# A gMLP output projection computed for two token blocks at a time with Strassen's seven products, in a one-core decoder trunk of split fp32 matmuls

## The chip, the core and the metric

The kernel runs on one core of a Trainium2 chip. The metric is the device time of one execution in microseconds. Three runs of the kernel before took 2581.13, 2582.24 and 2583.32 us; the median is 2582.24 us. All times below are of the kernel before.

## What is computed

A two-layer trunk for 2048 prompt tokens and 32 sample tokens with shared weights, model width 1024. Layer A (the one that changes) is a gated MLP over chunks of 128 positions:

```python
def chunk_gmlp(h, w_in, ln_g, ln_b, w_s, b_s, w_out):
    u, v, z = jnp.split(h @ w_in, 3, axis=-1)          # 3 x 2048 columns
    v = layernorm(v, ln_g, ln_b)
    ...
    s = jnp.einsum('hts,bnshd->bnthd', ws, vc) + bias  # mixes 128 positions, 8 heads
    gated = u * s.reshape(bn, seq_len, EXP_A) * jax.nn.silu(z)
    return gated @ w_out, v                            # (tokens, 2048) @ (2048, 1024)
...
x = x + rmsnorm(out, norm_post[i])
```

Layer B is an S5 state-space mixer and a GLU; the change leaves it as it is.

## The kernel before, in words

**Arithmetic.** Each fp32 product is made of three matmuls: an operand is split into a high part (ScalarE cast, L69) and a low part (VectorE subtraction, L70), and `mm3` (L62) accumulates hi·hi, hi·lo and lo·hi in a PSUM bank. The profile calls the weights' parts `whi` and `wlo`, those of the gate output `gs`, those of the normed input `hn`. `weight` (L72) loads 512 KB from DRAM into `wst` (2 buffers, SyncE's queue, L82) and splits it. PSUM has 6 banks `mm` for products and 2 `aux` for transposes.

**Order of layer A.** The prompt is four blocks `b` of 512 tokens; block 3 carries the 32 sample tokens too. For each block:
- `v_phase` (L250): v = hn·wv in four column groups n of 512, each group into four banks, copied by ScalarE into one `vq` tile of the pool `vg` (L274), with statistics by VectorE (L275).
- `uz_phase` (L329): 16 steps `db` of 128 features: u and z (112 matmuls with the spatial product, 12.0 us), then a = silu(z)·u (L344, L345), the spatial product `wsp`·`vq`, and gate output `gq` = spatial·a (L358, L365). `gq` is four tiles of `vg` (feature-major, 4 x 512 tokens each). In blocks 0 and 1 each step also makes tables for layer B (`cpow`, L681): GpSimd products, two small matmuls `aux<-oh,bsh`, a copy to `vt`, and for every second one eight DMAs `td<-vt` on SyncE's queue (L732).
- `out_phase` (L417): out = gated·w_out for the block through `tmajor` (L382): for each half h of the 1024 columns, 16 k of 128 features, four row tiles i, three matmuls of 128x512: 384 a block, in four banks. The four banks of a half are copied to `oq` by ScalarE and get their statistics by VectorE (`evac`, L154). Each operand tile `gs` is split just ahead of its use; the pool `gs` has two buffers.

The norm and transpose of the next block's input (`prep`, L126) run inside `out_phase` through a hook; the residual step of a block (`post`, L159: `xr` loaded, GpSimd or VectorE addition, store to x1d) runs in the next `v_phase`.

A scheduler in the framework sets the order on each engine; `later` and `behind` (L90 to L97) tie a load to an earlier weight load or split. Each queue is worked in order: what waits on SyncE's queue holds up every load behind it.

## Time and profile before

| | us |
|---|---|
| median of the runs | 2582.24 (2581.13 to 2583.32) |
| profiled execution | 2583.09 |
| its span | 2581.3 |
| TensorE (PE) busy | 2554.0, 99% |
| PE weight loads (PEld), beside PE | 2183.2, 85% |
| VectorE (DVE) busy | 1501.7, 58% |
| ScalarE (ACT) busy | 926.2, 36% |
| GpSimd (POOL) busy | 429.5, 17% |
| mean granted TensorE clock | 0.995 |

How to read it: the profile is of one execution, the span is what its trace covers, and the sum of the prediction is made against that execution's 2583.09 us. The matmuls are pipelined, so a duration of 0.39 us is that of one, and they start 0.227 us apart.

### The profile page before, as it was taken

The page shows a single profiled execution, that of the slowest core. Times are in us where ns is not written, and L with a number is a line of the kernel's source. Part 1 is how long each engine was busy: PE and PEld are TensorE (multiplying, and loading weights), DVE is VectorE, ACT ScalarE, POOL GpSimd, SP SyncE. Part 2 cuts the span into 40 slices and gives each one's busy share as a digit, 9 for nine tenths or more (in the row PEclk, how much of TensorE's full clock was granted, in tenths as well). Part 3 has the DMA queues.
Part 4 walks back from the last instruction along what each step waited for, and adds up shares of the span by engine and source line. Part 5 has one row for each costly group of instructions (what it writes and reads, how often), then busy time and mean ns, then how long its engine had stood idle before and what let it go on. Part 6 is the DMA issues. An engine that isn't in the chain of part 4 may idle for free.

```text
span 2581.3 us, 34682 instructions
## 1 busy us (share of the span) xinstructions
PE 2554.0 (99%) x13163; PEld 2183.2 (85%) x13163; DVE 1501.7 (58%) x2809; ACT 926.2 (36%) x1520; POOL 429.5 (17%) x624
## 2 busy tenths in 40 slices
PE   9999999999999999999999999999999999999998
PEld 8888888788888888887999877889888888888896
DVE  5955657745655755744633547417897346464645
ACT  3322443323443222532222344325556433434331
POOL 0345100455100000000100120000023212121220
PEclk9999999999999999999999999999999999999999
DMA  5333424343534454343322346537699545454533
GB/s 168 100 127 112 135 95 151 116 122 115 153 116 130 163 162 155 109 138 93 105 78 82 107 128 191 145 110 212 215 321 303 186 132 183 138 183 144 163 123 102
DMA packets 220631, 375.04 MB, mean 145 GB/s; under 512 B 59520, under 2 KB 135808, under 8 KB 220464
## 3 DMA queue, kind: packets, MB, share of 16 engines
q1 hardware_dynamic: 165728, 308.09, 37.6%
q0 software_dynamic: 13600, 39.90, 4.9%
q10 hardware_dynamic: 41136, 24.84, 3.4%
q8 instruction: 103, 1.69, 0.3%
q14 instruction: 64, 0.52, 0.1%
HBM read 311.64 MB, written 61.11 MB: 144 GB/s over the span
## 4 chain that ended last, share of the span: by engine, by line
PE 89%; DVE 5%; DMA 3%; issue 1%; ACT 1%; SPq 0%; POOL 0%; DVEq 0%; ACTq 0%; POOLq 0%
PE mm L60 85%; PE aux L60 3%; DMA x<-in_xp_dram 1%; DVE wlo L70 1%; PE aux L146 1%; DMA x<-x1d 1%; ACT junk L135 0%; DMA T<-td 0%; DMA Xo<-xd 0%; DVE nt L107 0%; DMA wst<-in_wib_dram 0%; ACT whi L69 0%; DVE o L175 0%; DVE nt L108 0%; DMA Xi<-xd 0%
## 5 line engine op out<-in xcount | busy, mean ns | idle before, releaser
L60 PE MATMUL mm<-hn,whi 128*128 128x512 f32 (+2 forms) x3840 | 1011.1, 351 | 0.0
L70 DVE TENSOR_TENSOR wlo<-wst,whi 128x1024 fp32r<-128x1024 f32 x400 | 516.3, 1292 | 536.0 <-ACT whi L69 520.6
L60 PEld LDWEIGHTS mm<-hn,whi 128*128 128x128 f32 x3840 | 671.6, 189 | 88.0 <-DVE a L345 0.2
L69 ACT CAST whi<-wst 128x1024 fp32r<-128x1024 f32 x400 | 419.7, 1050 | 860.4 <-PE mm L60 758.6
L60 PE MATMUL mm<-hn,wlo 128*128 128x512 f32 (+2 forms) x1920 | 673.2, 351 | 2.9 <-DVE wlo L70 2.9
L60 PEld LDWEIGHTS mm<-hn,wlo 128*128 128x128 f32 x1920 | 361.7, 188 | 48.4 <-DVE wlo L70 3.3
L60 PE MATMUL mm<-y,whi 128*128 128x512 f32 (+2 forms) x1280 | 333.8, 350 | 3.1 <-ACT y L69 2.9
L60 PE MATMUL mm<-whi,gs 128*128 128x512 f32 x1024 | 328.4, 393 | 2.2 <-ACT a L344 1.4
L60 PE MATMUL mm<-whi,hn 128*128 128x512 f32 x1024 | 324.4, 392 | 0.6 <-ACT hn L69 0.6
L60 PEld LDWEIGHTS mm<-y,whi 128*128 128x128 f32 x1280 | 224.7, 188 | 34.8 <-ACT y L69 3.6
L60 PEld LDWEIGHTS mm<-whi,gs 128*128 128x128 f32 x1024 | 191.6, 188 | 44.9 <-ACT a L344 1.7
L60 PEld LDWEIGHTS mm<-whi,hn 128*128 128x128 f32 x1024 | 192.6, 189 | 43.5 <-ACT hn L69 0.9
L60 PE MATMUL mm<-y,wlo 128*128 128x512 f32 (+2 forms) x640 | 223.1, 349 | 0.0
L60 PE MATMUL mm<-wlo,hn 128*128 128x512 f32 x512 | 200.2, 391 | 0.1
L60 PE MATMUL mm<-wlo,gs 128*128 128x512 f32 x512 | 199.8, 390 | 0.0
L70 DVE TENSOR_TENSOR gs<-gq,gs 128x512 fp32r<-128x512 f32 (+1 forms) x128 | 91.1, 714 | 133.7 <-ACT gs L69 133.4
L60 PE MATMUL mm<-whi,m 128*128 128x512 f32 x512 | 159.8, 389 | 0.0
L69 ACT CAST gs<-gq 128x512 fp32r<-128x512 f32 (+1 forms) x128 | 80.5, 629 | 190.3 <-PE mm L60 175.4
L60 PEld LDWEIGHTS mm<-y,wlo 128*128 128x128 f32 x640 | 120.8, 189 | 15.1
L60 PEld LDWEIGHTS mm<-wlo,hn 128*128 128x128 f32 x512 | 96.4, 188 | 21.5 <-DVE wlo L70 0.5
L358 DVE SCALAR_TENSOR_TENSOR gq<-mm,lng,Rp 128x512 f32<-128x512 f32 x64 | 47.9, 748 | 114.5 <-PE mm L60 114.5
L60 PEld LDWEIGHTS mm<-whi,m 128*128 128x128 f32 x512 | 96.1, 188 | 20.7
(287 smaller groups left out, 2624.0 us busy)
## 6 DMA issues: line engine op xcount, KB each, us to landing
wst<-in_wuz_dram SPq DMA_DIRECT2D x128, 512.0 KB
wst<-in_wv_dram SPq DMA_DIRECT2D x64, 512.0 KB
wst<-in_woa_dram SPq DMA_DIRECT2D x64, 512.0 KB
wst<-in_wg_dram SPq DMA_DIRECT2D x64, 512.0 KB
wst<-in_wib_dram SPq DMA_DIRECT2D x48, 512.0 KB
wst<-in_wob_dram SPq DMA_DIRECT2D x32, 512.0 KB
Xi<-xd SPq DMA_DIRECT2D x32, 272.0 KB
Xo<-xd SPq DMA_DIRECT2D x32, 272.0 KB
```

Of the source, the lines that this page charges most:

```text
L60: self.nc.tensor.matmul(out, lhsT, rhs, start=start, stop=stop)
L69: self.nc.scalar.copy(hi, src)
L70: return (e or self.nc.vector).tensor_tensor(lo, src, hi.bitcast(F32), SUB)
L146: nc.tensor.transpose(b[:, k * 128:k * 128 + P], x[:, o:o + 128], self.ident[:P, :P])
L358: nc.vector.scalar_tensor_tensor(g3, s3, self.lng[:, db:db + 1], R, MUL, ADD)
```

## The change

For the blocks (0,1) and (2,3), `out_pair` (new) replaces `out_phase`. The gate outputs of the two blocks are the upper and lower half of a 2x2 matrix of blocks (rows: even and odd block; columns: features k = 0..7 and 8..15), w_out a second one (features by column half). Strassen's scheme makes the four results from seven products instead of eight, each 8 k x 4 row tiles x 3 matmuls. In the order of the program, with the operand on the left:

| product | left operand | by | right operand |
|---|---|---|---|
| p1 | even(k) | loaded | w_out block |
| p6 | s2 = odd(k) - even(k) + odd(k+8) | GpSimd, then VectorE | `wtd` 2 |
| p2 | even(k+8) | loaded | w_out block |
| p7 | s3 = even(k) - odd(k) | GpSimd | `wtd` 1 |
| p5 | s1 = odd(k) + odd(k+8) | GpSimd, in place | `wtd` 0 |
| p3 | s4 = even(k) + even(k+8) - s1(k) | GpSimd, then VectorE | w_out block |
| p4 | odd(k+8) | in SBUF | `wtd` 3 |

- The even block's `gq` tiles go to DRAM (`gat`, `spill`, four writes of 1 MB a pair) and come back as tiles `ge` of 256 KB, 48 loads a pair, on SyncE's queue, in a ring of four. The sums are formed in the `ge` tiles.
- `combine_w` (new, in block 1, before its v_phase) makes the four sums of weights once on GpSimd: 32 loads of 256 KB, 32 additions of 128x512, 8 writes of 1 MB to `wtd`, all on GpSimd's queue, through tiles `tw` of the pool `vg`.
- A bank is no longer only copied: it is added by VectorE to the results it belongs to (p5 to two), and the statistics are then read from SBUF.
- `gs` has three buffers; `ge`, `gs` and the odd block's results are in a new pool `oc`, opened when the pair begins.
- The prep of blocks 1 and 3 moves into the `uz_phase` of blocks 0 and 2 (`prep_held`): ScalarE copies the transposes back to `x`, and `unhold` splits them into `hn` at the start of the odd block's `v_phase`. The residual steps of both blocks of a pair run after the pair: eight in block 2's `v_phase` (3, 3, 2), eight at the end of layer A.

In all 192 of the 1536 matmuls of 128x512 go, and 8 of the 64 weight loads of the four output projections.

```diff
+    def combine_w(self):
+        e, w = self.nc.gpsimd, self.I["woa"]
+        for kp in range(4):
+            for kk in range(2):
...
+                t = self.vg.tile([128, 4, 512], F32, tag="vg", name="tw", align_bytes=AL)
+                for i, (h, k) in enumerate(((0, kp), (1, kp), (1, kp + 4), (0, kp + 4))):
+                    e.dma_start(t[:, i], w[h, k][:, c])
+                b11, b12, b22, b21 = (t[:, i] for i in range(4))
+                e.tensor_tensor(b11, b12, b11, SUB)
+                e.tensor_tensor(b12, b22, b12, SUB)
+                e.tensor_tensor(b22, b22, b11, SUB)
+                e.tensor_tensor(b21, b22, b21, SUB)
+                e.dma_start(self.wtd[:, kp].rearrange("i p x -> p i x")[:, :, c], t)
+
+    def out_pair(self, s, hook):
...
+        oc = self.oc = self.tc.tile_pool(name="oc", bufs=2, reuse_waits="tile")
...
+        def even(k):
+            t = p.tile([128, 512], F32, tag="ge", name="ge", bufs=4)
+            self.later(t, self.gat[s][k])
+            return t
+        def s2(k):
+            t = even(k)
+            e.tensor_tensor(t, g(k), t, SUB)
+            v.tensor_tensor(t, t, g(k + 8), ADD)
+            return t
+        def s3(k):
+            t = even(k)
+            e.tensor_tensor(t, t, g(k), SUB)
+            return t
+        def s1(k):
+            e.tensor_tensor(g(k), g(k), g(k + 8), ADD)
+            return g(k)
+        def s4(k):
+            t, u = even(k), even(k + 8)
+            e.tensor_tensor(t, t, u, ADD)
+            v.tensor_tensor(t, t, g(k), SUB)
+            return t
...
+        for n, (pr, a, wsrc, asmp) in enumerate(plan):
+            bk = [self.bank() for _ in range(4)]
...
+            for kp in range(4):
+                hook(n * 4 + kp)
+                w = self.weight(wsrc(kp), (2, 512))
...
+                for k in ks:
+                    x = a(k)
+                    t = p.tile([128, 2, TB], F32R, tag="gs", name="gs", bufs=3, align_bytes=AL)
+                    self.split(t[:, 0], t[:, 1], x)
...
+                if kp < 3:
+                    for k in ks:
+                        for i in range(4):
+                            mm(i, k)
+                else:
+                    for i in range(4):
+                        for k in ks:
+                            mm(i, k)
+                        out(i, pr, bk[i])
...
             for b in range(NB):
+                if b % 2:
+                    self.unhold(hn, held)
+                    if b == 1:
+                        self.combine_w()
...
                 self.v_phase(b, hn, vhook)
```

The order on three queues, where the prediction speaks of it. First SyncE's queue at the end of block 1's `uz_phase`, where block 1's output projection (before) or the first pair (now) begins. `td<-vt` are the writes of the last tables, `wst` the weights, `x` the next block's input, `ge` the even block's gate output. Before:

```order
L97 DMA x<-in_xp_dram 128x1024 x2
L732 DMA td_92<-vt 16x4x128 x8
L82 DMA wst<-in_woa_dram 128x1024 x2
L732 DMA td_92<-vt 16x4x128 x8
L82 DMA wst<-in_woa_dram 128x1024 x11
```

And now:

```order
L97 DMA x<-in_xp_dram 128x1024 x2
L82 DMA wst<-in_woa_dram 128x1024
L912 DMA td_95<-vt 16x4x128 x8
L82 DMA wst<-in_woa_dram 128x1024
L82 DMA wst<-wtd 128x1024
L912 DMA td_95<-vt 16x4x128 x8
L97 DMA ge<-gat_74 128x512 x9
L82 DMA wst<-wtd 128x1024
```

The writes of the last tables stood behind the block's first four weight loads and nothing of its first products waited for them; now the first operand of the pair, `ge`, stands behind them, and it waits for all eight of SyncE's DMA counters as well, because `oc` takes over the memory of the tables' pool.

Second, VectorE in the first pair, from the end of p1 into p6 (`ge_5494` to `ge_5589` are p6's k = 0, 1, 2, ...; L478 is the VectorE part of s2, `gs<-ge` the low part of an operand):

```order
L478 TENSOR_TENSOR ge_5501<-ge_5501,gq_4460 128x512
L70 TENSOR_TENSOR gs_5453<-ge_5451,gs_5453 128x512
L478 TENSOR_TENSOR ge_5538<-ge_5538,gq_4460 128x512
L70 TENSOR_TENSOR gs_5498<-ge_5494,gs_5498 128x512
L70 TENSOR_TENSOR wlo_5535<-wst_5532,whi_5534 128x1024
L478 TENSOR_TENSOR ge_5545<-ge_5545,gq_4460 128x512
L478 TENSOR_TENSOR ge_5582<-ge_5582,gq_4880 128x512
L70 TENSOR_TENSOR gs_5505<-ge_5501,gs_5505 128x512
```

Before, VectorE had there one `wlo` and two `gs` for each pair of k and nothing else; now a sum stands between them for each k, and the sums of k = 3 and k = 4 (`ge_5545`, `ge_5582`) stand ahead of the low part of k = 1 (`gs_5505`).

Third, GpSimd's queue in the last step of block 0's `uz_phase` and the start of block 1's `v_phase`, where before it had only a `MEMSET vt` and one load (`oh` and `vt` belong to the tables, `tw` and `wtd` to `combine_w`; a tile's four additions are L441 to L444):

```order
L892 MEMSET vt_2722 16x4x112
L442 TENSOR_TENSOR tw_2870<-tw_2870 128x512
L442 TENSOR_TENSOR tw_2880<-tw_2880 128x512
L443 TENSOR_TENSOR tw_2850<-tw_2850 128x512
L443 TENSOR_TENSOR tw_2860<-tw_2860 128x512
L443 TENSOR_TENSOR tw_2870<-tw_2870 128x512
L443 TENSOR_TENSOR tw_2880<-tw_2880 128x512
```

```order
L444 TENSOR_TENSOR tw_2880<-tw_2880 128x512
L439 DMA tw_2890<-in_woa_dram 128x512
L445 DMA wtd_76<-tw_2850 128x4x512
L439 DMA tw_2890<-in_woa_dram 128x512 x3
L445 DMA wtd_76<-tw_2860 128x4x512
L445 DMA wtd_76<-tw_2870 128x4x512
L445 DMA wtd_76<-tw_2880 128x4x512
```

Ten additions and a load stand between that `MEMSET` and the first write; ScalarE's copy of block 1's first `vq` takes the memory of `tw_2870` and waits for the third write.

## Rows read from the trace of the kernel before

**Rows 1.** The page's busy times of the engines (us, share of the span, instructions).

```profile
PE 2554.0 (99%) x13163; PEld 2183.2 (85%) x13163; DVE 1501.7 (58%) x2809; ACT 926.2 (36%) x1520; POOL 429.5 (17%) x624
```

**Rows 2.** Busy time by stretch: the output projection of block 0, and two short stretches of layer B; columns: us from:to, length, busy us and instructions of PE, PEld, DVE, ACT, POOL, granted clock, DMA share, GB/s.

```profile
300.00:396.00 96.00, 95.92 (x444) 79.27 (x443) 56.12 (x85) 43.88 (x69) 1.03 (x2) 1.00 0.32 104
2120.00:2130.00 10.00, 10.00 (x46) 8.29 (x45) 7.20 (x9) 5.42 (x9) 1.29 (x1) 1.00 0.50 153
2446.00:2450.00 4.00, 4.00 (x34) 4.00 (x33) 2.43 (x4) 2.51 (x4) 2.37 (x3) 1.00 0.90 318
```

**Rows 3.** One piece of the chain of work that ended last, in the output projection of block 3 (start, us, what, number of matmuls).

```profile
1648.21 21.78 PE mm L60 x96
```

**Rows 4.** Groups of instructions by line and shape: count, busy us, mean ns of one, idle time before and what ended it.

```profile
L70 DVE TENSOR_TENSOR wlo<-wst,whi 128x1024 fp32r<-128x1024 f32 x400 | 516.3, 1292 | 536.0 <-ACT whi L69 520.6 <-PE aux L146 14.7
L70 DVE TENSOR_TENSOR gs<-gq,gs 128x512 fp32r<-128x512 f32 x96 | 68.1, 712 | 90.6 <-ACT gs L69 90.3
L157 DVE BATCH_NORM_STATS2 ost<-mm 128x6 f32<-128x512 f32 x56 | 35.4, 682 | 25.7 <-ACT oq L156 20.5 <-ACT o L156 5.1
L175 DVE SCALAR_TENSOR_TENSOR oq<-oq,rs,gpost 128x1024 f32<-128x1024 f32 x16 | 20.2, 1279 | 0.1
L176 DVE TENSOR_TENSOR xr<-xr,oq 128x1024 f32<-128x1024 f32 x16 | 19.5, 1221 | 0.3
L69 ACT CAST gs<-gq 128x512 fp32r<-128x512 f32 x96 | 59.8, 623 | 137.5 <-PE mm L60 128.1 <-DVE gq L365 9.0
L1061 POOL TENSOR_TENSOR gs<-zt,gs 128x512 f32<-128x512 f32 x24 | 32.0, 1334 | 194.1 <-ACT gs L1060 194.1
L709 POOL DMA_DIRECT2D cod<-co x32 | 23.9, 747 | 5.0 <-POOL co L707 5.0
```

**Rows 5.** Timeline of VectorE and GpSimd in layer B's GLU (start us, duration us, engine, line, operation).

```profile
2053.52 0.69 DVE L1062 TENSOR_TENSOR ga<-ga,gs 128x512 f32<-128x512 f32 x1
...
2056.13 1.41 POOL L1061 TENSOR_TENSOR gs<-zt,gs 128x512 f32<-128x512 f32 x1 [31.04 <-ACT gs L1060]
2056.31 1.79 DVE L1062 TENSOR_TENSOR ga<-ga,gs 128x512 f32<-128x512 f32 x1
```

**Rows 6.** Timeline at the end of block 1's `uz_phase`, all engines mixed; the last matmul of u and z is the first row, the first of the output projection the fourth.

```profile
676.57 0.39 PE L60 MATMUL mm<-hn,wlo 128*128 128x512 f32 x1
676.80 1.05 PE L60 MATMUL mm<-wsp,vq 128*128 128x128 f32 x8
...
677.61 0.71 PE L60 MATMUL aux<-oh,bsh 128*48 128x256 f32 x4
...
678.16 0.39 PE L60 MATMUL mm<-whi,gs 128*128 128x512 f32 x1
678.62 0.74 DVE L358 SCALAR_TENSOR_TENSOR gq<-mm,lng,Rp 128x512 f32<-128x512 f32 x1
679.29 1.22 DVE L70 TENSOR_TENSOR wlo<-wst,whi 128x1024 fp32r<-128x1024 f32 x1
...
683.09 2.46 DVE L140 SCALAR_TENSOR_TENSOR x<-x,rs,gpre 128x1024 f32<-128x1024 f32 x2
685.48 0.66 DVE L728 SCALAR_TENSOR_TENSOR vt<-ident,dT,vt 16x16 f32<-16x16 f32 x4
686.16 3.71 SPq L732 DMA_DIRECT2D td<-vt  x8
691.85 0.58 POOL L748 DMA_DIRECT2D ei<-ed  x1 [10.52 <-DMA td<-vt]
```

**Rows 7.** Loads of 256 KB: issue on SyncE's queue, and the ScalarE cast that waited for the first of them, at two places.

```profile
2123.01 0.97 SPq L1024 DMA_DIRECT2D yst<-yd  x2
2127.12 1.39 ACT L69 CAST y<-yst 128x512 fp32r<-128x512 f32 x2 [0.81 <-DMA yst<-yd]
...
2031.14 1.01 SPq L1024 DMA_DIRECT2D yst<-yd  x2
2036.66 1.37 ACT L69 CAST y<-yst 128x512 fp32r<-128x512 f32 x2 [6.10 <-DMA yst<-yd]
```

**Rows 8.** PE at the end of layer A, around its longest wait, sixteen transposes of `prep` a little later, and the busy times of the stretch around the wait (columns as in rows 2).

```profile
1576.32 0.61 PE L60 MATMUL mm<-hn,whi 128*128 128x512 f32 x2
1579.84 0.50 PE L60 MATMUL mm<-hn,wlo 128*128 128x512 f32 x1 [2.91 <-DVE wlo L70]
...
1581.27 1.05 PE L60 MATMUL mm<-hn,whi 128*128 128x512 f32 x2
...
1583.82 0.64 PE L60 MATMUL mm<-hn,whi 128*128 128x512 f32 x2
...
1587.96 1.91 PE L146 MATMUL aux<-ident,x 128*128 128x128 f32 x16
...
1579.00:1584.00 5.00, 4.16 (x11) 3.30 (x12) 5.00 (x14) 1.53 (x2) 0.00 (x0) 0.66 0.98 289
```

**Rows 9.** GpSimd around the end of block 0's `uz_phase`, and the last spatial product of that phase on PE.

```profile
265.45 0.47 POOL L712 MEMSET vt<- 16x448 f32 x1 [4.33 <-DMA td<-vt]
...
278.95 1.17 POOL L70 TENSOR_TENSOR oh<-co,oh 128x256 fp32r<-128x256 f32 x1 [10.85 <-ACT oh L69]
287.90 0.46 POOL L712 MEMSET vt<- 16x448 f32 x1 [7.79 <-DVE ms L136]
...
300.55 1.05 PE L60 MATMUL mm<-wsp,vq 128*128 128x128 f32 x8
```

More of the change, by code (lines that the diff above doesn't have):

```diff
@@ L334, in uz_phase @@
         for db in range(16):
+            if hook:
+                hook(db)
+            if b % 2 == 0 and db in (6, 10, 14):
+                self.spill(b, (db - 6) // 4)
             if db % 4 == 0:
@@ new lines, in out_pair @@
+        sts = [sts[:, i] for i in range(8)]
+        if smp:
+            sts.append(self.sm.tile([128, 2, 6], F32, tag="ost4", name="ost"))
+        c0, c1 = slice(0, 512), slice(512, 1024)
+        gq = self.gq
+        g = lambda k, c=slice(0, TB): gq[k // 4][:, k % 4, c]
+        sc = slice(TB, TX)
+        def even(k):
[7 more added lines that the diff above has]
+            return t
@@ new lines, in fold, with out @@
+        def fold(b):
+            t = self.tmp.tile([128, TX], F32, tag="a", name="a")[:NS, :512]
+            self.fold_sample(t, b)
+            return t
+        def out(i, pr, bk):
+            st = lambda r, h, x: v.bn_stats(sts[4 * r + i][:, h], x)
+            t0, t1, b0, b1 = T[i][:, c0], T[i][:, c1], B[i][:, c0], B[i][:, c1]
+            if pr == 1:
+                nc.scalar.copy(t0, bk)
+            elif pr == 6:
+                v.tensor_tensor(t1, bk, t0, ADD)
+            elif pr == 2:
+                v.tensor_tensor(t0, bk, t0, ADD)
+                st(0, 0, t0)
+            elif pr == 7:
+                v.tensor_tensor(b0, bk, t1, ADD)
+            elif pr == 5:
+                v.tensor_tensor(t1, bk, t1, ADD)
+                v.tensor_tensor(b1, bk, b0, ADD)
+                st(1, 1, b1)
+            elif pr == 3:
+                v.tensor_tensor(t1, bk, t1, ADD)
+                st(0, 1, t1)
+            else:
+                v.tensor_tensor(b0, b0, bk, SUB)
+                st(1, 0, b0)
@@ L448, in fin @@
         def fin():
             if smp:
-                yield from self.post([os_], [sts[4][:NS]], NS, self.gpost, [I["xs"]], [self.x1s])
-            yield from self.post([oq[i // 2][:, i % 2] for i in range(4)], sts[:4], 128, self.gpost,
-                                 [I["xp"][b, i] for i in range(4)], [x1[i] for i in range(4)], 1 if smp else 2)
+                yield from self.post([os_], [sts[8][:NS]], NS, self.gpost, [I["xs"]], [self.x1s])
+            for r, rows in ((0, T), (1, B)):
+                b = 2 * s + r
+                yield from self.post(rows, sts[4 * r:4 * r + 4], 128, self.gpost, [I["xp"][b, i] for i in range(4)],
+                                     [self.x1c(b)[i] for i in range(4)], 1 if smp else 2)
@@ L495, in vhook @@
             def vhook(n):
-                if b:
-                    with self.behind():
-                        next(fin)
+                if b == 2:
+                    for _ in range((3, 3, 2, 0)[n]):
+                        with self.behind():
+                            next(fin)
+                if b % 2 and n == 0:
+                    self.spill(b - 1, 3)
                 if b == 0 and n == 1:
@@ L506, in layer_a @@
             for b in range(NB):
+                if b % 2:
+                    self.unhold(hn, held)
+                    if b == 1:
+                        self.combine_w()
+                    else:
+                        smp = self.tc.tile_pool(name="smp", bufs=1, reuse_waits="tile")
+                        self.smp = smp.__enter__()
+                        self.stk = self.smp.tile([128, 8, 2 * NS], F32R, name="stk", align_bytes=AL)
+                        for e in range(2):
+                            self.nc.gpsimd.tensor_copy(self.stk[:, :, e * NS:e * NS + NS], hn[:, e, :, TB:TX])
                 self.v_phase(b, hn, vhook)
@@ L509, in layer_a @@
                     self.tables_e()
+                if b == 2:
+                    self.oc.__exit__(None, None, None)
+                if b % 2 == 0:
+                    held, jobs = self.prep_held(b + 1, hn)
+                    gen = self.steps(jobs)
+                    self.uz_phase(b, hn, lambda db: next(gen, None) if db in (8, 10, 12, 13) else None)
+                    continue
                 self.uz_phase(b, hn)
@@ L1138, in build @@
             t = lambda n, shape: dr.tile(shape, F32, name=n)
+            self.gat = [t(f"gat{i}", [16, 128, TB]) for i in range(2)]
+            self.wtd = t("wtd", [4, 4, 128, 1024])
             self.bsd = t("bsd", [128, 64, 16])
```

115 lines of the change are left out of this document (81 added, 34 removed).

## The prediction, made before the change was run

> **What bounds the kernel now.** I read the busy times first: the reader is to see that PE is busy 99% of the span and that the other engines have a third or more of their time free [rows 1]. Then the stretch of one of the four output projections, which the change rewrites: PE is busy 95.92 of 96.00 us there, at full granted clock, with VectorE at 56 and GpSimd at 1 [rows 2]. So the time of such a stretch is its matmuls times their pace, and nothing else is late in it. The chain of waits gives the pace: 96 matmuls in 21.78 us [rows 3], 0.227 us each, 2.72 us for the 12 matmuls of one k, 21.8 us for a product of 8 k. Last I read the ends of the neighbouring phases and each new kind of operation's nearest row, since a kernel with PE full can only lose by new waits.
>
> **What it removes.** 192 matmuls x 0.2269 us = **43.5 us**, all on the path. The eight weight loads and splits that go lay beside PE: nothing.
>
> **Entry of pair 0: +16 us (10 to 18).** Let Z be the end of block 1's last u,z matmul, 676.96 [rows 6]. Before, the projection started at 678.16 without a gap, since its operand lay in SBUF. Now p1's first operand is a `ge` load behind the last eight `td` writes on SyncE's queue, and it waits for their landing. Those writes wait for `vt`: VectorE finished it at 686.14 after two scalings of `x` (2.46 us), which now stand earlier, so at about 683.7, Z+6.7. Eight issues take 3.71, and the last landed 1.98 after its issue (691.85 - 689.87): Z+12.4. A 256 KB load on this queue took 4.1 us from issue to the cast that waited (2123.01 to 2127.12) [rows 7], the cast takes 0.62 [rows 4]: Z+17.1. PE would have started at Z+1.2: 15.9 us, of which 1.9 are filled by the 16 transposes that stand there anyway [rows 8]. After a stall the clock comes back late: after the 2.91 us wait of rows 8, ten matmuls took 3.98 us (1579.84 to 1583.82) where 2.27 is their pace, at a granted clock of 0.66. That is 1.7 more: 15.7, say 16. Lower end: the operand is ready at Z+12; upper: the landing of 5.5 us in rows 7.
>
> **Entry of pair 1: +4 us (0 to 7).** No tables are written there, so `ge` is loaded early. The first `gs` low parts stand on VectorE behind the tail of the last gate step and behind the sample's splits; in rows 6 that tail ends some 5 us after the phase's last matmul. PE has transposes and spatial products for half of it: 2.5 us of wait and 1.7 of slow clock.
>
> **Products with sums: +12 us for both pairs (0 to 28).** The rows first: a VectorE addition of two SBUF tiles took 0.69 alone and 1.79 beside a GpSimd addition that had begun 0.18 earlier; it ended 0.56 after that one's end [rows 5], so the two go one after the other. Per k, p6 and p3 need GpSimd 1.33, VectorE 0.69 for the sum, 0.71 for `gs`, and half a `wlo` of 1.29 [rows 4]: 3.4 us against PE's 2.72. p7 and p5 need 2.7 and just fit; p1, p2 and p4 need 1.4. Summed over a pair that is 130 of 152 us, so it is a matter of lookahead, which the `ge` ring of four sets. In p6 VectorE has the sums of k = 3 and 4 ahead of the low part of k = 1. The sum of k = 4 needs the buffer of k = 0, free when its low part is made: then 0.4 of issue, 4.1 of landing, 1.33 and 0.69 of sums and up to 0.7 of waiting for the port, so k = 1 is some 7 us behind k = 0, while PE asks for it after 2.72; by the order k = 0 is some 2 us ahead of PE, my estimate. Late by about 2.5. In p3 each k takes two `ge`: four buffers hold two k, and one turn is landing + 3.7 us (issue, two sums, cast, low part) against 5.44 of PE for two k. Two of the four turns are loaded ahead during p5: 2 x (4.1 + 3.7 - 5.44) = 4.7, less about 1 for the third `gs` buffer: 3.7. Per pair 6, for two pairs 12. With the 5.5 us landing of rows 7: p6 3.9, p3 6.5, each with 1.7 of slow clock, 14 a pair. With all lookahead holding: 0. I take the 4.1, landed at a DMA share of 0.50 [rows 2]; these products move 4 to 6.3 MB per 21.8 us, 192 to 289 GB/s; the trace has reached 318 at a share of 0.90 [rows 2], so they have room, if not much in p3.
>
> A page of the Trainium skill would make this term nothing: SBUF — State Buffer, The DMA setup-cost knee, fits a transfer as about 2 us plus bytes over 436 GB/s, an estimate of 2.6 us for 256 KB, and by it p3's turn would be 6.3 and the sum some 10 us lower. The 4.1 and 5.5 us of rows 7 disagree with it, so I keep the rows.
>
> **unhold: +1.5 us.** In two odd blocks the first matmuls now wait for the first cast, 0.62 [rows 4], and part of the first low part, 0.7, after the last matmul that reads the old `hn`, less the spatial products that stand between; before there was no gap. Bounds 0 and 3, by how much of both the spatial products (1.05) hide.
>
> **combine_w: 0 (0 to +10).** In block 0's last step the tables' `MEMSET` ran at 287.90 [rows 9], and 10 additions of 1.33 stand between it and the writes: they end at about 302, or 305 with the port shared; the last spatial product ran at 300.55. Four issues of 0.75 and 3 MB of writes at 200 to 300 GB/s put the third write's landing some 18 to 20 us after the phase's end, and ScalarE's first `vq` copy needs it at 22 (one column group, 96 matmuls). Just in time.
>
> **At nothing, with its cover.** Evictions: VectorE takes 0.68 for each added bank instead of ScalarE, 8.2 us at the end of p5 (two additions and statistics for four banks); two spare banks cover 1.36 us each, without them 1.4 us a bank. It waits for PE four times in a row at a product's end, with the next product's third `gs` queued behind; that one is due 5.4 us later. Spills: four 1 MB writes a pair on SyncE's queue during the gate phase, where DMA has room. Posts: three in one 21.8 us group of block 2's v_phase cost VectorE 7.5 (1.28 + 1.22 each) [rows 4] beside some 7.6 of its own. At layer A's end eight instead of four posts stand beside layer B's first products, where four already made the wait of 2.91 [rows 8]; now `wlo` stands between them: 0, at worst 5.
>
> **Sum.** -43.5 + 16 + 4 + 12 + 1.5 = -10.0, from the profiled 2583.09: 2573.1; that execution is 0.85 above the median, so **2572.2 us** against 2582.24.
>
> **Rivals.**
> - *Lookahead holds.* Landings stay near 4 us or less and p6 and p3 lose nothing: -43.5 + 16 + 4 + 1.5 = -22, 2560; with an entry of 10 us 2554. For it: only 130 of 152 us of port work a pair. Against it: the order in p6, where two sums stand ahead of a due operand.
> - *Slower: the `ge` ring sets the pace of p6 and p3.* Place: 16 k a pair. With landings of 5.5 us at the entry too the sum is -43.5 + 17.4 + 4 + 1.5 + 28 = +7.4, 2590. It decides from a landing of about 5 us on, where p6 and p3 together lose 11 a pair. For it: 289 GB/s asked in p3, and the 5.5 of rows 7. Against it: most landings lie near 4.
> - *Slower: combine_w is late.* Block 1's first `vq` copy waits for `wtd`, and PE for a bank. Sixteen loads stand ahead of the additions on GpSimd's queue. Begun after the `MEMSET` of 265.45, they are over at 278 at 0.75 us an issue [rows 4, 9]; at four times that they end at 314, some 12 us after the phase, the additions 20 us later, and the copy is 25 to 30 us late: about 2600. The trace's 32 such issues, in the gate phases beside a busy VectorE, speak against it. Here the Trainium skill speaks against the change: SBUF — State Buffer, A bandwidth-pool intuition that's wrong, has a GpSimd-queue DMA of some 620 ns take some 3100 ns beside a VectorE `tensor_copy`, because the descriptors cannot be written meanwhile; the mean of 747 ns in rows 4 does not show it.
> - That it leaves out no work: the built order has 192 matmuls less, so no chance.
>
> **Chances.** The forecast's case 0.45 (2563 to 2582), lookahead holds 0.18, ring sets the pace 0.25, combine_w late 0.07, others 0.05. About 0.2% (5.2 us) is what a measurement of this kernel can tell from no change: bounds 2577.1 and 2587.4. Faster: 0.34 of the forecast's case, 0.18 and 0.02: 0.54. Within: 0.11 + 0.04 + 0.01 = 0.16. Slower: 0.21 + 0.06 + 0.03 = 0.30. The range goes from 2552, just under lookahead holding with a short entry, to 2600, past the ring's 2590 and up to combine_w's, which leaves out about 0.1.
>
> **What would show it.** Right: a PE gap of about 14 us at pair 0's entry, ended by ScalarE's cast of `gs` and that by `ge`; small gaps in p6 and p3 ended by VectorE's low part of `gs`, with `ge` landing at 4 us; PE at 21.8 us for p1, p2, p4, p5, p7; no gap in block 1's v_phase. Wrong: p6 or p3 over 30 us; a wait of `vq` on `wtd`; no gap at the entry; or p7 and p5, which I cost at nothing, over 23 us.

## The result, and the profile after

The changed kernel takes **2595.72 us** (median of 6 runs, 2588.37 to 2600.74) against 2581.99 for the kernel before on the same chips: a ratio of 1.005 [1.0034, 1.0067]. It is slower; 2572.2 was forecast. The profiled execution took 2600.74 us and is the slowest of the six; its span is 2598.6, 17.3 more than the 2581.3 of before, where the medians are 13.7 apart. What follows explains the 17.3 of these two executions.

The page's busy times of after answer to [rows 1]:

```profile
PE 2531.0 (97%) x12971; PEld 2155.0 (83%) x12971; DVE 1591.5 (61%) x2917; ACT 911.1 (35%) x1522; POOL 560.5 (22%) x690
```

The 192 matmuls are gone (13163 to 12971), but PE is busy only 23.0 us less, since part of the rest ran at a lower clock or a slower pace, and it is idle 40 us more. GpSimd is 131 us busier: its sums take 143 (41 in `combine_w`, 102 in the pairs) and `combine_w`'s DMA issues 24, while 36 of casts for the sample are gone. The waits of PE in after (engine, line and tile that waited, what ended it: us in total, times, longest) name the suspects:

```profile
PE mm L60 <- DVE wlo L70: 15.3, 6, 4.9
PE mm L60 <- ACT gs L69: 11.5, 7, 6.1
PE aux L147 <- DVE x L141: 5.6, 1, 5.6
...
PE aux L147 <- DVE vt L906: 3.8, 1, 3.8
```

Next I cut both spans at the same places (from a phase's first matmul to the next one's):

| stretch | before | after | difference |
|---|---|---|---|
| start, v_phase and uz_phase of block 0 | 301.67 | 305.23 | +3.6 |
| v_phases of blocks 1 to 3 and all output projections | 658.37 | 641.62 | -16.8 |
| uz_phase of block 1 and the entry of pair 0 | 198.21 | 208.12 | +9.9 |
| uz_phase of block 2 | 188.56 | 196.73 | +8.2 |
| uz_phase of block 3 | 213.17 | 213.77 | +0.6 |
| layer B's first matmul to the span's end | 1021.3 | 1033.1 | +11.8 |

The uz_phases of blocks 0 and 2 now hold 32 transposes each, 3.8 us at the pace of [rows 8], and the entry of pair 0 sixteen, that stood in the second line before; they cancel. The busy times by stretch of after, the answer to [rows 2] (columns as there), are the v_phase of block 1, the entry with block 1's uz_phase, pair 0, and the start of layer B:

```profile
305.23:417.53 112.30, 96.72 (x386) 77.30 (x385) 75.01 (x140) 27.48 (x40) 61.89 (x78) 0.89 0.59 212
417.53:625.65 208.12, 197.71 (x954) 166.04 (x952) 122.04 (x221) 65.23 (x111) 92.00 (x136) 0.97 0.41 121
625.65:789.58 163.93, 158.70 (x689) 128.97 (x689) 124.70 (x159) 66.24 (x98) 50.38 (x32) 0.98 0.52 167
...
1565.20:1660.00 94.80, 84.09 (x378) 69.11 (x378) 67.76 (x145) 37.97 (x75) 0.00 (x0) 0.95 0.80 238
```

**The largest loss is the first row.** The v_phase has the same 386 matmuls in e1 (below), where nothing of `combine_w` runs, and takes 87.09 us there:

```profile
305.32:392.41 87.09, 87.09 (x386) 72.09 (x385) 47.71 (x128) 27.08 (x39) 21.99 (x37) 1.00 0.37 118
```

Here it takes 112.3: +25.2. PE is idle 15.6 of them, and with its clock at 0.89 of full speed the same matmuls take 9.6 longer. GpSimd is busy 61.89 us. What happens shows in the timeline of after, VectorE beside GpSimd, in three places (start us, duration us, engine, line, operation):

```profile
293.54 2.52 POOL L442 TENSOR_TENSOR tw<-tw 128x512 f32<-128x512 f32 x2
293.81 13.28 DVE L70 TENSOR_TENSOR wlo<-wst,whi 128x1024 fp32r<-128x1024 f32 x1
296.03 5.02 POOL L443 TENSOR_TENSOR tw<-tw 128x512 f32<-128x512 f32 x4
301.01 4.99 POOL L444 TENSOR_TENSOR tw<-tw 128x512 f32<-128x512 f32 x4
...
352.00 5.61 DVE L782 TENSOR_TENSOR ztb<-zta 64x64 f32<-64x64 f32 x1
352.50 1.28 POOL L441 TENSOR_TENSOR tw<-tw 128x512 f32<-128x512 f32 x1
353.75 1.28 POOL L443 TENSOR_TENSOR tw<-tw 128x512 f32<-128x512 f32 x1
355.00 1.28 POOL L442 TENSOR_TENSOR tw<-tw 128x512 f32<-128x512 f32 x1
356.25 1.28 POOL L441 TENSOR_TENSOR tw<-tw 128x512 f32<-128x512 f32 x1
...
366.10 1.28 POOL L441 TENSOR_TENSOR tw<-tw 128x512 f32<-128x512 f32 x1
366.23 9.97 DVE L70 TENSOR_TENSOR wlo<-wst,whi 128x1024 fp32r<-128x1024 f32 x1 [0.25 <-ACT whi L69]
```

A `wlo` of 1.22 us takes 13.28: it began 0.27 after the first of ten additions in a row and ended 1.1 after the tenth. A 64x64 operation takes 5.61 beside four additions. VectorE did not get its turn after one addition, as in [rows 5]; here it waited until the whole run was over. (In the third place it waited for five additions, with DMA issues and small operations between them.) PE waits behind it (four of the stretch's five waits):

```profile
307.14 0.50 PE L60 MATMUL mm<-wlo,hn 128*128 128x512 f32 x1 [1.52 <-DVE wlo L70]
...
311.14 1.22 PE L60 MATMUL mm<-whi,hn 128*128 128x512 f32 x2 [3.03 <-DVE hn L70]
...
345.13 0.79 PE L60 MATMUL mm<-wlo,hn 128*128 128x512 f32 x1 [3.66 <-DVE wlo L70]
376.26 0.80 PE L60 MATMUL mm<-wlo,hn 128*128 128x512 f32 x1 [4.87 <-DVE wlo L70]
```

The first two stand behind the `wlo` of 13.28, the last behind that of 9.97. The third is less direct: its `wlo` took a normal 1.21, but came late behind small operations of VectorE, of which two took 2.38 and 1.81 us beside GpSimd's work instead of 0.2.

**Entry of pair 0**, from the timelines of several engines, the answer to [rows 6, 7]:

```profile
609.81 1.05 PE L60 MATMUL mm<-wsp,vq 128*128 128x128 f32 x8
615.11 1.94 PE L147 MATMUL aux<-ident,x 128*128 128x128 f32 x8 [3.79 <-DVE vt L906]
615.91 5.08 SPq L912 DMA_DIRECT2D td<-vt  x8
622.37 1.76 SPq L97 DMA_DIRECT2D ge<-gat  x4
624.98 1.29 ACT L69 CAST gs<-ge 128x512 fp32r<-128x512 f32 x2 [4.78 <-DMA ge<-gat]
625.65 0.79 PE L60 MATMUL mm<-whi,gs 128*128 128x512 f32 x1 [6.08 <-ACT gs L69]
```

The chain is the forecast's: with Z = 609.97 the first `td` write goes out at Z+5.9, the `ge` load at Z+12.4, PE starts at Z+15.7.

**The end of layer A**, PE, the answer to [rows 8]:

```profile
1583.94 0.50 PE L60 MATMUL mm<-hn,wlo 128*128 128x512 f32 x1 [1.53 <-DVE wlo L70]
1593.26 0.79 PE L60 MATMUL mm<-hn,wlo 128*128 128x512 f32 x1 [3.59 <-DVE wlo L70]
1616.55 1.97 PE L147 MATMUL aux<-ident,x 128*128 128x128 f32 x8 [5.59 <-DVE x L141]
```

Before, there was one wait of 2.91; now there are three, 10.7 us in all. Layer B's first 448 matmuls are the same in every kernel (384 of its first product, 64 transposes), so the time that they take measures this end. Before, then after (columns as in [rows 2]): 98.7 and 109.0 us.

```profile
1559.98:1658.72 98.74, 95.83 (x449) 79.73 (x447) 64.26 (x156) 39.35 (x76) 2.88 (x2) 0.98 0.65 182
1565.47:1674.44 108.97, 98.26 (x448) 81.11 (x447) 71.11 (x150) 43.39 (x86) 0.00 (x0) 0.95 0.79 227
```

**Block 2's uz_phase** has no wait in either kernel, and yet its matmuls are slower. The groups by shape between 860 and 1045 us of before and 880 and 1075 of after (count, busy us, mean ns):

```profile
L60 PE MATMUL mm<-hn,whi 128*128 128x512 f32 x502 | 156.1, 392 | 0.0
```

```profile
L60 PE MATMUL mm<-hn,whi 128*128 128x512 f32 x508 | 160.3, 396 | 0.0
```

At a granted clock of 1.00 in both, 16 steps of 11.79 us became 12.04: +4.0 beside the transposes. Block 2's v_phase, also without a wait, takes 88.76 us for its 386 matmuls, 1.7 more than e1's 87.09 above for block 1. What differs is that `hn` of block 2 is now 544 columns wide, made ready for block 3's sample; a row of it is 2176 bytes instead of 2048.

### The profile page after: what moved, and what is told of

Read it like the earlier page. It is cut to its first block, busy times and chain, and to the rows that moved or that the text cites. A ratio compares the mean times of both kernels' runs of the same rounds, so it can differ in the third digit from the quotient of the medians.

```text
span 2598.6 us, 34769 instructions
## 1 busy us (share of the span) xinstructions
PE 2531.0 (97%) x12971; PEld 2155.0 (83%) x12971; DVE 1591.5 (61%) x2917; ACT 911.1 (35%) x1522; POOL 560.5 (22%) x690
## 4 chain that ended last, share of the span: by engine, by line
PE 85%; DVE 6%; DMA 5%; issue 1%; ACT 1%; POOL 1%; SPq 0%; DVEq 0%; ACTq 0%; POOLq 0%
PE mm L60 81%; PE aux L60 3%; DVE wlo L70 2%; DMA ge<-gat 1%; PE aux L147 1%; DMA x<-x1d 1%; DMA wst<-in_wib_dram 1%; DMA x<-in_xp_dram 0%; ACT whi L69 0%; POOL ge L492 0%; DMA T<-td 0%; DMA Go<-gd 0%; DMA x1d<-xr 0%; DMA zta<-in_ldtg_dram 0%; DMA wst<-in_wv_dram 0%
## 5 line engine op out<-in xcount | busy, mean ns | idle before, releaser
L70 DVE TENSOR_TENSOR wlo<-wst,whi 128x1024 fp32r<-128x1024 f32 x392 | 536.9, 1371 | 534.8 <-ACT whi L69 524.8
L60 PEld LDWEIGHTS mm<-hn,whi 128*128 128x128 f32 x3840 | 671.3, 188 | 90.6 <-ACT hn L69 0.3
L69 ACT CAST whi<-wst 128x1024 fp32r<-128x1024 f32 x392 | 410.9, 1049 | 904.3 <-PE mm L60 771.8
L60 PE MATMUL mm<-whi,hn 128*128 128x512 f32 x1024 | 331.6, 399 | 6.3 <-DVE hn L70 3.0
L60 PE MATMUL mm<-whi,gs 128*128 128x512 f32 x896 | 283.4, 394 | 14.1 <-ACT gs L69 11.5
L60 PEld LDWEIGHTS mm<-whi,gs 128*128 128x128 f32 x896 | 168.9, 189 | 55.2 <-ACT gs L69 14.8
L60 PE MATMUL mm<-wlo,hn 128*128 128x512 f32 x512 | 204.2, 399 | 10.2 <-DVE wlo L70 10.2
L60 PE MATMUL mm<-wlo,gs 128*128 128x512 f32 x448 | 175.2, 392 | 0.0
L60 PEld LDWEIGHTS mm<-wlo,hn 128*128 128x128 f32 x512 | 98.3, 192 | 34.4 <-DVE wlo L70 12.4
L60 PE MATMUL mm<-wlo,m 128*128 128x512 f32 x256 | 99.7, 389 | 0.0
L60 PEld LDWEIGHTS mm<-wlo,gs 128*128 128x128 f32 x448 | 84.7, 189 | 17.6
```

Of the source, the lines that this page charges most:

```text
L60: self.nc.tensor.matmul(out, lhsT, rhs, start=start, stop=stop)
L69: self.nc.scalar.copy(hi, src)
L70: return (e or self.nc.vector).tensor_tensor(lo, src, hi.bitcast(F32), SUB)
```

## The experiments

Twelve kernels ran; each ratio is to runs of the kernel before on the same chip (median 2580.7 to 2581.62).

| run | median us | ratio, 95% | v_phase of block 1 | layer B's first 448 | last output matmul to PE's last |
|---|---|---|---|---|---|
| before | 2581.99 | | | 98.7 | 1012.1 |
| after | 2595.72 | 1.0050 [1.0034, 1.0067] | 112.3 | 109.0 | 1023.2 |
| e1_no_sums | 2570.94 | 0.9961 [0.9948, 0.9974] | 87.1 | 110.7 | 1021.6 |
| e2_transfers_only | 2576.67 | 0.9981 [0.9972, 0.9991] | 92.9 | 106.6 | 1017.8 |
| e3_sums_on_vector | 2577.41 | 0.9982 [0.9973, 0.9991] | 89.0 | 114.4 | 1027.0 |
| e4_before_wide_hn | 2586.12 | 1.0021 [1.0012, 1.0031] | | 98.1 | 1011.4 |
| e5_entry | 2579.43 | 0.9987 [0.9976, 0.9998] | 92.3 | 118.2 | 1030.6 |
| e6_posts_early | 2577.22 | 0.9986 [0.9977, 0.9995] | 92.1 | 110.0 | 1022.5 |
| e7_pitch | 2572.39 | 0.9963 [0.9950, 0.9976] | 90.6 | 107.5 | 1017.0 |
| e8_together | 2587.48 | 1.0018 [1.0009, 1.0027] | 90.8 | 110.9 | 1023.5 |
| e9_own_queue | 2571.97 | 0.9962 [0.9949, 0.9976] | 90.6 | 107.5 | 1021.3 |
| e10_alternate | 2580.19 | 0.9997 [0.9988, 1.0006] | 96.0 | 110.3 | 1023.1 |
| e11_no_steps | 2567.89 | 0.9944 [0.9926, 0.9962] | 90.9 | 102.4 | 1013.8 |
| e12_no_vector_steps | 2567.40 | 0.9941 [0.9920, 0.9963] | 91.5 | 103.2 | 1015.6 |

The three right columns are of the one profiled execution of each run. The last one holds all of layer B and is what some expectations call the time to the span's end; the 4 us by which e7 and e9 differ in it arise over 260 us into layer B. Even the first 448 take 106.6 to 114.4 us in after, e1, e2, e3 and e10, which have the same program there, so small differences in either column show nothing.

**e1, no `combine_w`.** The products read plain weights in place of the sums.

```diff
-        wt = lambda i: lambda kp: self.wtd[i, kp]
+        wt = lambda i: lambda kp: I["woa"][i % 2, kp + 4 * (i // 2)]
...
-                    if b == 1:
-                        self.combine_w()
-                    else:
+                    if b != 1:
```

> The changed kernel without combine_w: no loads, additions or writes for the sums of weights, and the four products that used them read plain weight blocks (so the output is not the projection). Theory P (port: GpSimd's runs of additions keep the operand port, and VectorE's low parts of the weights wait for a whole run): block 1's v_phase falls from 112 us to 88 to 90, no wait of PE there over 2 us, total 22 to 26 us less, about 2571 as a median. Theory D (DMA: the 16 MB of loads and writes delay the weights): the same fall, so this run alone doesn't tell P from D. Theory U (unhold and the moved prep cost it): v_phase stays over 105, total within 5 of the changed kernel.

Measured 2570.94, 24.8 us under after, and the v_phase 25.2 shorter: without `combine_w` the change is a gain of 0.4%, so this part alone turns it into a loss. Which of its parts does it, this run can't tell.

**e2, its transfers without its additions**, and **e3, its additions on VectorE.**

```diff
-                e.tensor_tensor(b11, b12, b11, SUB)
...
-                e.tensor_tensor(b21, b22, b21, SUB)
```

> The changed kernel with combine_w's 32 loads and 8 writes, without its 32 additions (so the weights' sums are not made). Theory P: VectorE's wlo in block 1's v_phase takes 1.2 to 1.5 us each and the phase 88 to 93 us, total 18 to 25 us under the changed kernel. Theory D: the weights still land late, PE waits for ScalarE's cast of the weights, the phase stays at 105 to 112 and the total within 6 us.

```diff
-                e.tensor_tensor(b11, b12, b11, SUB)
...
-                e.tensor_tensor(b21, b22, b21, SUB)
+                self.nc.vector.tensor_tensor(b11, b12, b11, SUB)
...
+                self.nc.vector.tensor_tensor(b21, b22, b21, SUB)
```

> The changed kernel with the 32 additions of combine_w on VectorE instead of GpSimd; everything else as it is. Theory P: 32 x 0.69 = 22 us of VectorE spread over the end of block 0's gate phase and block 1's v_phase, none of it waiting for the port: the phase 89 to 95 us, total 15 to 24 us under the changed kernel, about 2575. Theory D: phase 105 to 112, total as changed. If the additions' place in VectorE's order is what matters (they stand ahead of the splits of hn), the gain is under 12 us with waits at the phase's start.

The v_phase of e3 has the same transfers and the same 32 additions, on the other engine. The stretch of e2, then of e3 (columns as in [rows 2]):

```profile
304.16:397.10 92.94, 89.85 (x387) 72.78 (x386) 50.58 (x133) 29.03 (x43) 31.63 (x48) 0.98 0.55 190
```

```profile
305.26:394.27 89.01, 87.43 (x387) 72.03 (x385) 57.64 (x147) 27.61 (x40) 28.37 (x47) 1.00 0.57 195
```

The transfers cost 5.9 us over e1 (5.7 by the medians), the additions on GpSimd 19.4 more (19.1 by the medians). On VectorE the same additions are 32 x 0.68 = 22 us of work and cost little: the phase takes 89.0 us in e3 and 90.6 to 92.3 in the seven other kernels that have them all there (it starts up to 4 us later in some of these), against e2's 92.9 without any, and the medians of e2 and e3 are 0.7 apart. VectorE had the time for them; what it lacked beside GpSimd's runs was its turn.

**e10, every second addition on VectorE.** It asks whether the amount of GpSimd's work costs the time, or its runs.

```diff
-                e.tensor_tensor(b12, b22, b12, SUB)
+                self.nc.vector.tensor_tensor(b12, b22, b12, SUB)
...
-                e.tensor_tensor(b21, b22, b21, SUB)
+                self.nc.vector.tensor_tensor(b21, b22, b21, SUB)
```

> The change with every second addition of combine_w (L442 and L444) on VectorE and the others on GpSimd, so that GpSimd's next addition of a tile waits for one of VectorE's and never more than two stand in a row without such a wait; the transfers are the same. First v_phase of block 1: 112.3 us with all 32 on GpSimd, 89.0 with all on VectorE, 92.9 with none. Theory run (an operation of VectorE that reads two SBUF tiles waits until GpSimd has no further addition to start, however many stand in a row): with runs of one or two nothing waits over some 3 us, so 89 to 93. Theory amount (each GpSimd addition costs VectorE its own length, in whatever order): 16 instead of 32 additions, half of the loss, 100 to 103.

96.0 us: outside both ranges. With half of the additions on GpSimd, 3.1 over e2's transfers are left of 19.4, and 7.0 over e3 are left of 23.3: a sixth to a third, not a half. By the medians it is 3.5 of 19.1 over e2. Its timeline, VectorE and GpSimd:

```profile
338.75 1.26 POOL L443 TENSOR_TENSOR tw<-tw 128x512 f32<-128x512 f32 x1 [0.32 <-DVE tw L442]
338.81 1.28 DVE L727 SCALAR_TENSOR_TENSOR zta<-zta 64x64 f32<-64x64 f32 x1
339.97 2.49 POOL L441 TENSOR_TENSOR tw<-tw 128x512 f32<-128x512 f32 x1
340.12 1.21 DVE L70 TENSOR_TENSOR wlo<-wst,whi 128x1024 fp32r<-128x1024 f32 x1
```

The small operation waits for one addition and gets its turn behind it; then the next addition takes 2.49 and `wlo` its usual 1.21. Here they do alternate. So most of the cost comes from the length of the runs and not from the amount, though no run shows what lets VectorE in: the second addition followed the first at once here too.

**e4, the kernel before with block 2's `hn` 544 columns wide.**

```diff
-        hn = pool.tile([128, 2, 8, TX if b == NB - 1 else TB], F32R, tag=tag, name="hn",
+        hn = pool.tile([128, 2, 8, TX if b == NB - 1 else TX if b == NB - 2 and pool is self.hnp else TB], F32R, tag=tag, name="hn",
```

> The kernel before with one size changed: block 2's hn tile has 544 columns in each k (pitch 2176 bytes) instead of 512 (2048), as the changed kernel has it; the same columns are read. Theory A (pitch or alignment of the moving operand sets PE's pace): a step of block 2's gate phase takes 12.04 us instead of 11.79, the whole phase 4.0 us more and the total about 2586. Theory B (something else in the changed kernel slows that phase, its DMA traffic or the place of other tiles): 11.79 and no change, 2582.

Block 2's uz_phase takes 192.5 instead of 188.56 us, the median 4.9 more. The group between 860 and 1045 us of e4, to be set beside before's 392 ns:

```profile
L60 PE MATMUL mm<-hn,whi 128*128 128x512 f32 x494 | 155.9, 396 | 0.0
```

Same work, same order, no waits. The output projection and v_phase just before grow by 1.5 as well (178.43 to 179.88). The only edit is the width of the tile; that it also moves other tiles in SBUF was not separated.

**e7, e3 with the sample's columns in a tile of their own**, so that block 2's `hn` is 512 wide again.

```diff
+                        for e in range(2):
+                            self.nc.gpsimd.tensor_copy(hn[:, e, :, TB:TX], hs[:, e])
...
-                    hn, jobs = self.prep_jobs(2, I["xp"][2], None, self.gpre, self.hnp, "hn", 2, TX)
+                    hn, jobs = self.prep_jobs(2, I["xp"][2], None, self.gpre, self.hnp, "hn", 2)
```

> The weight sums on VectorE as in e3, and block 2's hn with its pitch of 2048 bytes: the sample columns are kept in a tile of their own and copied into a wider hn when block 3 begins. By e4 a step of block 2's gate phase takes 11.79 instead of 12.04 us (apart from the transposes), total 4 us under e3, about 2573; if the copy at block 3's start is waited for, block 3's v_phase grows by up to 2.

Block 2's v_phase takes 87.03 instead of 88.76 and its uz_phase 194.2 instead of 196.7; in the latter a wait of 1.0 for ScalarE's first cast of block 3's `hn`, now a tile of its own, gives back part of the 4.0. The kernel takes 2572.39: 5.0 less than e3, and faster than both kernels.

**e5, e3 with p4 first** (its operand lies in SBUF) and the odd block's results allocated behind the first operands, against the wait at pair 0's entry.

```diff
-        plan = ((1, even, low, lambda k: g(k, sc)),
+        plan = ((4, lambda k: g(k + 8), wt(3), None),
+                (1, even, low, lambda k: g(k, sc)),
...
-                (3, s4, lambda kp: I["woa"][1, kp + 4], ssum),
-                (4, lambda k: g(k + 8), wt(3), None))
+                (3, s4, lambda kp: I["woa"][1, kp + 4], ssum))
```

> The weight sums on VectorE as in e3, and the pair begun with p4, whose operand lies in SBUF (its result is first copied and subtracted later, in p7), with the odd block's result tiles taken from the pool after the operand tiles, so that these don't wait for the last table writes. Theory E (the entry waits for the table writes and a load): the gap of 3.8 + 1.0 + 6.1 us at pair 0's start falls to under 3, total 9 to 13 us under e3, about 2566. Theory M (the wait moves: the second operand or p1's first load inherits it): a wait of 5 us or more shows up inside p4 or at p1's start and the total stays within 5 us of e3.

The entry wait falls from 6.08 to 1.20:

```profile
601.25 0.80 PE L60 MATMUL mm<-whi,gs 128*128 128x512 f32 x1 [1.20 <-ACT gs L69]
```

But layer B's first 448 matmuls now take 118.2 us, 3.7 more than in e3; p3, the longest product, is now the pair's last, though no run shows that this is why. In time nothing is gained: 2579.43 beside e3's 2577.41.

**e6, e3 with the residual steps of the sample and block 2 called inside p4.**

```diff
+                if smp and pr == 4:
+                    for _ in range(2 if kp == 0 else 1):
+                        with self.behind():
+                            next(gen)
```

> The weight sums on VectorE as in e3, and in the second pair the residual steps of the sample rows and of the even block, whose sums are complete after p3, run during p4 instead of after it; four instead of eight are left for layer A's end. Theory W (eight residual steps on VectorE and their loads on SyncE's queue delay layer B's first weights): PE's waits after the pair fall from about 10 us to the 3 of the kernel before, total 6 to 10 us under e3, about 2569. Theory X (p4 pays for them): p4 grows by 4 us or more and the total stays within 4 of e3.

No change (2577.22), but nothing was tested either: in the trace VectorE does block 2's first four L179 at 1541.58 us, in e3 at 1539.87. Only four loads on SyncE's queue changed places.

**e8, all at once**: p5 first, late results, narrow `hn`, early steps, sums on VectorE.

```diff
+        plan = ((5, s1, wt(0), None),
...
-                (5, s1, wt(0), None),
```

> All of it: weight sums on VectorE, the pair begun with a product whose operand lies in SBUF (p5, in place of p4 in e5, with its sum in the two results added in p7, so that p4 stays last), operand tiles ahead of the result tiles, residual steps of the even block in p4, block 2's hn at the pitch of 2048 bytes. If the costs add up: 2577.4 - 10 - 8 - 4 = about 2555, range 2550 to 2562, 1% under the kernel before. If they share a cause, or the products with sums take the slack that the waits gave them, 2562 to 2572.

2587.48, slower than each part. Pair 0 takes 171.4 instead of 163.9 us, and pair 1 182.6 instead of 173.1. In pair 0 it is p7, in which VectorE now adds p5's result as well (24.7 instead of 22.0), and p3 behind it (34.6 instead of 27.6). PE waits for VectorE to empty banks of p2 and p7 (L514, L517), which it never did in after. The waits in the 185 us around pair 0:

```profile
PE mm L60 <- DVE gs L70: 5.3, 3, 3.6
...
PE mm L60 <- DVE oq L517: 2.3, 1, 2.3
PE mm L60 <- DVE oq L514: 1.7, 1, 1.7
```

**e9, e7 with the `xr` loads of pair 1 on GpSimd's queue.**

```diff
-            self.later(x, res[i])
+            nc.gpsimd.dma_start(x, res[i]) if fast == 1 else self.later(x, res[i])
```

> The kernel of e7_pitch (additions of combine_w on VectorE, sample's hn in its own tile), and the eight xr loads of the second pair issued on GpSimd's queue instead of SyncE's. Nothing else moves: PE, VectorE and ScalarE have the same instructions in the same order. Theory W (at layer A's end the weights and the x1d loads of layer B stand on SyncE's queue behind xr loads that wait for a buffer of the x pool): the wst loads go out in time, the PE waits ended by wlo and by VectorE's x at that end go, and from the last matmul of the second pair to the span's end it takes 1012 to 1014 us as in the kernel before, 3 to 5 less than e7's 1017.0; the median comes to about 2568. Theory V (VectorE's eight residual steps, 1.28 + 1.22 us and four at 4.86, and not the queue, hold that end): the waits stay, 1016 to 1018, median 2572.

Theory W falls. Between the sample's `xr` and layer B's `gpre` SyncE's queue now holds weights alone, and the waits stay: 0.57, 3.44 on `wlo` and 3.84 on `x` (in e7 0.56, 3.44, 4.14). Layer B's first 448 matmuls take 107.5 us in both, and the median, 2571.97, is no different. VectorE of e9 at that place:

```profile
1559.27 4.87 DVE L179 SCALAR_TENSOR_TENSOR oq<-oq,rs,gpost 128x1024 f32<-128x1024 f32 x4
1564.06 2.35 DVE L180 TENSOR_TENSOR xr<-xr,oq 128x1024 f32<-128x1024 f32 x2
1566.33 1.22 DVE L70 TENSOR_TENSOR wlo<-wst,whi 128x1024 fp32r<-128x1024 f32 x1
```

**e11, e9 without block 2's residual steps**, and **e12, without VectorE's part of them.**

```diff
+                if smp and r == 0:
+                    for i in range(4):
+                        nc.scalar.dma_start(self.x1c(b)[i], rows[i])
+                        yield
+                    continue
```

> The kernel of e9_own_queue without the four residual steps of block 2 in the second pair: no xr loads, no L179 and no L180 for them, the rows of oq are written to x1d as they are (so x1 of block 2 lacks its normalisation and its residual). What is left beside layer B's first weights is what the kernel before had there: the sample's step and four of block 3. Theory V (twice as many residual steps on VectorE and in the four buffers of x as before make layer A's end longer): the waits on wlo and on VectorE's x there fall to one of some 3 us, and from the last matmul of the second pair to the span's end it takes 1012 to 1014 us, against 1017.0 in e7 and 1021.3 in e9. Rival: the end is longer because p4's results are last and the matmuls of layer B come in another order; then 1017 to 1021 stays. Median by V 2563 to 2568, by the rival 2572.

```diff
+                if smp and r == 0:
+                    for i in range(4):
+                        x = self.xp.tile([128, D], F32, tag="x", name="xr")
+                        nc.gpsimd.dma_start(x, I["xp"][b, i])
+                        nc.scalar.dma_start(self.x1c(b)[i], x)
...
```

> As e11, but block 2's four x rows are still loaded into buffers of x and written from there to x1d, with no L179 and L180 (x1 of block 2 is then x alone). VectorE is relieved of 9.7 us, the four buffers are taken as before, but no longer held until VectorE comes. If VectorE's time is what delays layer B's start, or the time for which it holds the buffers, it is as quick as e11, 1012 to 1014 us from the last matmul of the pair to the span's end. If the buffers and their transfers alone delay the loads of x1d, it stays at 1016 to 1021.

Layer B's first 448 matmuls take 102.4 and 103.2 us against 107.5 in e9 and e7, and the medians are 4.1 and 4.6 below e9's. First e9, then e11:

```profile
1540.92:1648.42 107.50, 99.25 (x448) 81.82 (x447) 71.48 (x150) 42.95 (x87) 2.65 (x5) 0.95 0.77 230
1540.86:1643.26 102.40, 96.52 (x449) 80.54 (x448) 62.33 (x141) 43.58 (x86) 0.53 (x1) 0.97 0.71 201
```

All the waits on `wlo` and `x` there go; one on ScalarE's cast of a weight takes their place (5.9 and 6.2). In e11 that cast stands behind ScalarE's work on the rows loaded from x1d, for which ScalarE waits 6.59. The x1d loads of layer B go out ten us earlier (1570.22 in e9, 1560.10 in e11).

So eight residual steps instead of four cost some 4 to 5 us at that end: all ten kernels with eight lie at 106.6 us or above there, and the medians agree, though the intervals of the ratios touch. With the buffers and transfers kept but VectorE relieved, e12 is nearly as quick as e11: it is VectorE's time, or the time for which it holds the buffers, which the two runs don't separate.

## Why the prediction was wrong, step by step

**The failed step is combine_w: 0 (0 to +10); measured +25.2**, 15 past its bound. The forecast asked when the additions end and who needs their result, and there it was right: they ended at 306, forecast 302 or 305; nothing waited for `wtd`. It did not ask what they do to VectorE meanwhile. [rows 5] shows one GpSimd addition beside one of VectorE, one after the other, and "305 with the port shared" took it that they alternate. Shown by the rows of after: beside ten additions in a row VectorE waited for all ten. Shown by e1, e2, e3: the additions on GpSimd are 19 to 23 of the 25.2, the rest is the transfers. Of the forecast's own signs, "no gap in block 1's v_phase" is the one that failed.

The Trainium skill (SBUF — State Buffer, Who interferes with whom) has VectorE and GpSimd share a port pair as an exclusive lock for one whole instruction. The 1.28 us in e10 agrees; the 13.28 does not: by that rule one addition of 1.28 and its own 1.22 make 2.5, an estimate. The forecast's late-combine_w rival came out near in time (2600) by luck, through another mechanism: GpSimd's load issues took 4.25 us for eight, 0.53 each, not four times their usual; that rival is wrong.

**Layer A's end: 0, at worst 5; measured +11.8**, of it 10.2 in layer B's first 448 matmuls. "Eight instead of four posts" was named, and "`wlo` stands between them: 0" is what failed: VectorE still does four L179 in a row, twice. e9 rules out the queue; e11 and e12 show that block 2's four steps are 4 to 5 of e9's 8.8 there. The rest stays open.

**Not in the sum: block 2's wide `hn`, +5.7**, 4.0 in its uz_phase and 1.7 in its v_phase, shown by e4 and e7. And a gain: the kernel before lost PE time at the start of block 1's uz_phase, three waits on `vq` of 2.6 us and then a slow clock. The changed kernel has neither, and takes 4.6 less from there to Z. That stretch before:

```profile
480.00:500.00 20.00, 17.43 (x72) 13.87 (x71) 19.22 (x29) 5.48 (x9) 17.18 (x29) 0.91 0.31 101
```

**Matmuls, -43.5: right.** Without waits a product takes 21.8 to 22.0 us (p4, p5, p7 of pair 0).

**Entry of pair 0, +16: right in its chain, 1 too long.** PE starts 14.5 later than before. As in the forecast, 1.9 go off for the 16 transposes, which stood elsewhere before; here they took 3.9 (1.94 and 1.97 for eight, twice their time in [rows 8]). And 2.4 of slow clock come on: p1 took 24.2, and from 625.6 to 630 the granted clock was 0.50, the 1.2 GHz level, after 6.08 us in which PE did nothing. 15.0 in all. The load landed after 2.61 us, not 4.1; by the Trainium skill's page (SBUF — State Buffer, The DMA setup-cost knee), which I had set against [rows 7], the estimate is 2.6, and here the trace agrees.

**Entry of pair 1, +4: the waits came, but not as a loss.** They are 1.55 and 0.25, 1.8 in all, without a slow clock. The kernel before waited just as long at that place (1.45 and 0.38), which the forecast did not look up, so the stretch grew by 0.6 only:

```profile
1453.65 0.50 PE L60 MATMUL mm<-whi,gs 128*128 128x512 f32 x1 [1.45 <-ACT a L344]
```

**Products with sums, +12: size about right, cause only in part.** In pair 0 p6 took 23.0 without its two transposes (+1.2, forecast 2.5) and p3 27.6 (+5.8, forecast 3.7); in pair 1 the waits are 1.03 and 1.48. The forecast laid p3 on the `ge` ring and costed p5's evictions at nothing. The busy times of after in p3's first 12 us show VectorE (third engine) full:

```profile
739.30:745.00 5.70, 5.61 (x25) 4.32 (x23) 5.70 (x11) 2.66 (x4) 1.24 (x1) 1.00 0.32 119
745.00:751.00 6.00, 5.46 (x24) 4.53 (x25) 6.00 (x8) 1.21 (x2) 1.81 (x1) 1.00 0.55 175
```

In it lie p5's eight additions and four statistics, 8.2 us, and p3's sums and low parts queue among them. p3's two longest waits, 1.71 and 1.25, come later, behind GpSimd's sums that wait for `ge`, in part issued late and landing in some 2 to 4 us. How much is the one and how much the other no run told apart.

**unhold, +1.5: measured 0.** Block 1's v_phase starts 0.97 after the last matmul of u and z, where the output projection before started after 0.96, and in e1 it runs its 87.09 us without a wait.

**The ledger:** -10.0 forecast, +25.2 (combine_w), +11.8 (end), +5.7 (width), -4.6 (uz start), -1.0 and -3.4 (both entries), -2.4 (products), -1.5 (unhold): +19.8, against the 17.3 measured. The 2.5 between them are spread over the stretches and were not assigned. e7, with the additions off GpSimd and `hn` narrow, takes 2572.39, what was forecast, but by luck: there the slower end of layer A is set off by smaller terms that came out below the forecast.

## What to carry to other kernels

Before work is moved to an idle GpSimd, count what VectorE reads from two SBUF tiles at that time, and how long GpSimd's run is: here the price was up to the run's whole length on VectorE's next operation, not one operation's. An engine's free time is of no use where the other engine's run keeps it from its turn. Look up whether a wait that you add to the sum is there already in the kernel before. Where two fixes seem to add up, run them together: e5's entry and e8's sum gave back elsewhere all that they won.
